# One token in eight of the gated one-hots on ScalarE, and sorted picks looked up among 8 and 16 entries

## The chip, the cores and the metric

The kernel runs on one core of a Trainium2 chip. The metric is the device time of one execution in microseconds, the median of several runs. TensorE (PE) multiplies matrices, VectorE (DVE) and ScalarE (ACT) work element by element, GpSimd (POOL) does so too and issues indirect loads, SyncE (SP) issues loads and stores. The engines run side by side, each in the order of its own instructions, and wait for each other through semaphores.

## The reference

The model is one encoder block with a gated mixer, an attention and a retrieval over 128 x 128 single-neuron experts (PEER). The change is in the retrieval alone. For 512 tokens and 8 heads two lists of 128 scores are reduced to their best 16, the sums of pairs to the best 16 pairs, and the expert is read from the two lists:

```python
s1, i1 = lax.top_k(s[:, :, 0], PEER_TOPK)
s2, i2 = lax.top_k(s[:, :, 1], PEER_TOPK)
cand = (s1[..., :, None] + s2[..., None, :]).reshape(PEER_TOKEN_BLOCK, PEER_HEADS, PEER_TOPK * PEER_TOPK)
sc, ci = lax.top_k(cand, PEER_TOPK)
e = (jnp.take_along_axis(i1, ci // PEER_TOPK, axis=-1) * N_KEYS
     + jnp.take_along_axis(i2, ci % PEER_TOPK, axis=-1))
g = jax.nn.softmax(sc, axis=-1)
u = expert_u[e]
act = jax.nn.gelu(jnp.einsum('td,thkd->thk', xb, u).astype(jnp.float32))
return jnp.einsum('thk,thkd->td', (g * act).astype(xb.dtype), expert_v[e])
```

## The kernel before

The order of each engine's instructions is that in which the program writes them; nothing reorders them later. Three of the four blocks of 128 tokens go the dense way: the hidden values of all 128 x 128 experts are computed, 128 experts at a time (a "u": a load `uraw`, its rounded part `uhi` by ScalarE, the rest `ulo` by GpSimd or, from the weights stage on, by VectorE, 24 matmuls into `pu` at L200, a GELU at L759), weighted by a table of each token's gates, and multiplied with the experts' output rows (L1007). The fourth block gathers its 128 picked experts row by row (L953 and after). `ahead(n, limit)` writes the next n matmuls of the u's between other work; `los()` writes the splits on VectorE that are due. Buffers of `uraw`, `uhi`, `ulo` and `pu` are two each.

`decode` turns the numbers of the 16 picked pairs into two lists of expert indices. The row and the column of a pair (`rw`, `cl`, 0 to 15) are copied 16 times by ScalarE (L676), compared with 0 to 15 (L683), multiplied by the sorted list's indices (L685) and summed by halves (L690, L692). It runs five times: for 3, 3 and 2 heads of the three dense blocks (n = heads x blocks = 9, 9, 6), between about 310 and 397 us, and for 4 and 4 heads of the fourth block (n = 4), between 617 and 647 us.

`turn(b)` transposes a block's indices and gates so that the 128 picks of a token lie on the partitions. The weights stage (about 400 to 545 us) then goes through 48 rounds of 8 tokens. For each, `hots` writes two one-hots of 128 per token on VectorE (`ohb`, L846, 16 rows of 128) and multiplies those of the first index with the gate, split into two 16-bit parts (`oha`, L850, 16 rows of 128). TensorE multiplies them, 16 matmuls per round (L887), to a token's table of 128 x 128 weights; ScalarE evacuates it (L867) and issues the stores. `hots` runs two rounds ahead and has three buffers of each one-hot; `acc` has four buffers, of which a round takes two. Each round has ten matmuls of u's behind its own.

The list is sorted: the pick with rank k (from 0) can only have a row or column of at most k, since every pair in front of it in both directions scores at least as high.

Of the kernel before, what the change touches and what calls it, by code (L numbers as in the profile page):

```python
# [8 lines left out]
F32 = mybir.dt.float32  # L9
# [17 lines left out]
TOPK = 16  # L27
# [17 lines left out]
def peer_block(ctx: ExitStack, tc: tile.TileContext, A, out):  # L45
# [597 lines left out]
    def decode(pool, lists, ci, outs):  # L643
# [3 lines left out]
        tl = lambda nm, dt: pool.tile(PK, dt, name=nm)  # L647

# [23 lines left out]
        wide = [128, n, TOPK, TOPK]  # L672
        ohs = []
        for r in (rw, cl):
            oh = pool.tile([128, nh, nb, TOPK, TOPK], BF16, name="oh", bufs=3 if pool is rt else 2)
            S.copy(oh.rearrange("p h b r c -> p (h b) r c"),  # L676
                   r.rearrange("p h b k -> p (h b) k")[:, :, :, None].to_broadcast(wide))
            ohs.append(oh)
        yield
        io = iota_b[:, None, None, 0:TOPK].to_broadcast(wide)  # L680
        o4 = [oh.rearrange("p h b r c -> p (h b) r c") for oh in ohs]
        for o in o4:
            V.tensor_tensor(o, o, io, op=ALU.is_equal)  # L683
        for p, o in enumerate(o4):
            V.tensor_tensor(o, o, fi.rearrange("p h b s k -> p (h b) s k")[:, :, p, None, :].to_broadcast(wide),  # L685
                            op=ALU.mult)
        yield
        for w in (8, 4, 2):
            for o in o4:
                V.tensor_tensor(o[:, :, :, 0:w], o[:, :, :, 0:w], o[:, :, :, w:2 * w], op=ALU.add)  # L690
        for oh, o in zip(ohs, outs):
            V.tensor_tensor(o, oh[:, :, :, :, 0], oh[:, :, :, :, 1], op=ALU.add)  # L692
# [15 lines left out]
    HG = (3, 3, 2)  # L708
    route = [rt.tile([128, DB, H, TOPK], F32, name=f"route{i}") for i in range(3)]
# [34 lines left out]
    def pick_head(h):  # L744
# [3 lines left out]
        for n in HG:  # L748
            if h == h0 + n - 1:
                steps.append(decode(rt, dense[1][:, h0:h0 + n], ci[:, h0:h0 + n], [r[:, h0:h0 + n] for r in by_head]))  # L750
            h0 += n
# [57 lines left out]
    def turn(b):  # L809
# [16 lines left out]
        gw = rt.tile([128, 16, 2, 8, 2], F16, name="gw", bufs=2)  # L826
        V.tensor_copy(gw[:, :, 0], gT)
        V.tensor_tensor(gw[:, :, 1], gT, gw[:, :, 0], op=ALU.subtract)
        tsc[b] = (idx, gw)
# [8 lines left out]
    def hots(t8):  # L838
# [3 lines left out]
        idx, gw = tsc[b]  # L842
# [6 lines left out]
        wide = [128, 2, 8, NK // 2, 2]  # L849
        V.tensor_tensor(a.rearrange("p (s t) (k two) -> p s t k two", s=2, two=2),  # L850
# [356 lines left out]
```

## Time and profile before

| | us |
|---|---|
| median of 3 runs | 1499.62 (1498.49 to 1500.58) |
| the profiled execution | 1503.86 |
| its span, first to last instruction | 1501.6 |
| TensorE busy | 1459.0 |
| VectorE busy | 1161.3 |
| ScalarE busy | 640.3 |
| GpSimd busy | 281.0 |

The profile is of one execution, which was a little slower than the median of the three. An engine counts as busy while an instruction of it runs. The mean granted clock of TensorE is 0.993 of full speed. In the rows below a line number is one of the kernel before; "out<-in" are the tiles that an instruction writes and reads; a releaser in brackets is what ended the engine's idle time before an instruction.

### The profile page before, as it was taken

The numbers are of one execution on the slowest core, as the hardware profiler recorded it, in microseconds if no ns is written. First come the engines' busy times: TensorE is split into PE (matmuls) and PEld (weight loads), VectorE is DVE, ScalarE is ACT, GpSimd is POOL, SyncE is SP. The second block draws the span as 40 slices with busy tenths as digits, with TensorE's granted clock in tenths as the row PEclk, the third lists the DMA queues.
The fourth block names the chain that finished last, engine by engine and source line by source line (L and its number), as shares of the span: only waits on it lengthen the run. The fifth ranks groups of instructions, "written<-read, shape, count | busy, mean of one in ns | idle before, by whom it ended". The sixth has DMA issues, their size and how long they took to land.

```text
span 1501.6 us, 21590 instructions
## 1 busy us (share of the span) xinstructions
PE 1459.0 (97%) x7945; PEld 1296.2 (86%) x7945; DVE 1161.3 (77%) x2415; ACT 640.3 (43%) x1088; POOL 281.0 (19%) x222
## 2 busy tenths in 40 slices
PE   8999999998999999899999999999999999999997
PEld 6878988888888899789999999999999999987785
DVE  4745554799999958879888888888888888877765
ACT  5455753344555543343333333333333333324334
POOL 0140002445400000012222212222212221211002
PEclk9999999999999999999999999999999999999999
DMA  6331032332366775389999999899999999988764
GB/s 218 105 101 51 22 127 91 95 95 90 113 255 265 253 274 203 105 308 354 340 338 326 331 328 336 322 327 315 337 335 322 323 321 327 324 284 292 253 199 166
DMA packets 129641, 359.31 MB, mean 239 GB/s; under 512 B 9216, under 2 KB 60672, under 8 KB 113024
## 3 DMA queue, kind: packets, MB, share of 16 engines
q1 hardware_dynamic: 104048, 198.54, 40.3%
q0 software_dynamic: 18432, 134.23, 23.6%
q10 hardware_dynamic: 7056, 25.18, 4.2%
q8 instruction: 62, 1.02, 0.3%
q14 instruction: 43, 0.35, 0.1%
HBM read 327.50 MB, written 30.41 MB: 238 GB/s over the span
## 4 chain that ended last, share of the span: by engine, by line
PE 72%; DVE 13%; DMA 7%; ACT 3%; issue 3%; POOL 1%; ACTq 0%; SPq 0%; DVEq 0%; POOLq 0%
PE pu L200 31%; PE acc L1007 27%; PE acc L251 6%; DMA vraw<-in_uv_dram 4%; DVE ohb L846 3%; DVE ulo L180 2%; DVE oha L850 2%; DVE vlo L80 1%; DMA uraw<-in_uT_dram 1%; ACT vhi L79 1%; PE tr L729 1%; PE tr L433 1%; PE pu L251 1%; POOL ulo L180 1%; PE acc L446 1%
## 5 line engine op out<-in xcount | busy, mean ns | idle before, releaser
L200 PE MATMUL pu<-h2T,uhi 128*128 128x384 f32 (+2 forms) x2336 | 452.4, 343 | 4.9 <-ACT act L759 2.4
L200 PEld LDWEIGHTS pu<-h2T,uhi 128*128 128x128 f32 x2336 | 410.6, 189 | 21.3 <-ACT uhi L169 3.0
L953 POOL DMA_INDIRECT uv<-in_uv_dram,ei x128 | 168.3, 1315 | 844.0 <-DVE xlast L968 352.0
L80 DVE TENSOR_TENSOR vlo<-vraw,vhi 128x1024 fp32r<-128x1024 f32 x128 | 156.8, 1225 | 155.7 <-ACT vhi L79 155.7
L79 ACT CAST vhi<-vraw 128x1024 fp32r<-128x1024 f32 x128 | 134.6, 1051 | 287.2 <-issue 174.7
L200 PE MATMUL pu<-h2T,ulo 128*128 128x384 f32 (+2 forms) x1168 | 236.2, 342 | 7.4 <-DVE ulo L180 5.2
L1007 PE MATMUL acc<-vhi,wahi 128*128 128x512 f32 x768 | 239.4, 392 | 2.2 <-ACT wahi L79 2.2
L1007 PE MATMUL acc<-vlo,wahi 128*128 128x512 f32 x768 | 239.1, 392 | 0.4
L1007 PE MATMUL acc<-vhi,walo 128*128 128x512 f32 x768 | 238.2, 391 | 0.0
L200 PEld LDWEIGHTS pu<-h2T,ulo 128*128 128x128 f32 x1168 | 204.9, 189 | 13.8 <-DVE ulo L180 6.4
L169 ACT CAST uhi<-uraw 128x1024 fp32r<-128x1024 f32 x144 | 150.7, 1047 | 63.1 <-DMA uraw<-in_uT_dram 49.8
L1007 PEld LDWEIGHTS acc<-vlo,wahi 128*128 128x128 f32 x768 | 144.4, 189 | 33.9 <-DVE vlo L80 2.4
L1007 PEld LDWEIGHTS acc<-vhi,walo 128*128 128x128 f32 x768 | 144.2, 188 | 31.6 <-DVE walo L80 0.7
L968 DVE SCALAR_TENSOR_TENSOR xlast<-uv,dot,xlast 128x1024 f32<-128x1024 f32 x128 | 164.5, 1285 | 4.5
L1007 PEld LDWEIGHTS acc<-vhi,wahi 128*128 128x128 f32 x768 | 143.2, 188 | 27.3 <-ACT wahi L79 3.5
L959 DVE SCALAR_TENSOR_TENSOR uv<-uv,h 128x1024 f32<-128x1024 f32 x128 | 153.7, 1219 | 9.5 <-DMA uv<-in_uv_dram,ei 9.5
L180 DVE TENSOR_TENSOR ulo<-uraw,uhi 128x1024 fp32r<-128x1024 f32 x116 | 141.6, 1220 | 22.6 <-ACT uhi L169 22.3
L759 ACT ACTIVATE act<-pu 128x384 f32<-128x384 f32 x128 | 62.9, 491 | 220.6 <-PE pu L200 220.2
L180 POOL TENSOR_TENSOR ulo<-uraw,uhi 128x512 fp32r<-128x512 f32 x56 | 81.3, 1475 | 209.3 <-PE acc L251 106.3
L79 ACT CAST wahi<-wa 128x384 fp32r<-128x384 f32 x128 | 65.3, 510 | 41.2 <-DVE wa L992 41.2
L992 DVE TENSOR_TENSOR wa<-act,wt 128x384 f32<-128x384 f32 x128 | 70.6, 551 | 2.2 <-DMA wt<-wd 2.1
L80 DVE TENSOR_TENSOR walo<-wa,wahi 128x384 fp32r<-128x384 f32 x128 | 70.7, 553 | 0.6 <-ACT wahi L79 0.6
(250 smaller groups left out, 1475.7 us busy)
## 6 DMA issues: line engine op xcount, KB each, us to landing
uraw<-in_uT_dram SPq DMA_DIRECT2D x128, 512.0 KB, 6.1
vraw<-in_uv_dram SPq DMA_DIRECT2D x128, 512.0 KB, 5.6
wd<-wst ACTq DMA_DIRECT2D x48, 512.0 KB, 2.8
wt<-wd SPq DMA_DIRECT2D x32, 768.0 KB, 11.2
wraw<-in_w_in_dram SPq DMA_DIRECT2D x19, 512.0 KB, 3.7
uraw<-in_w_q_dram SPq DMA_DIRECT2D x16, 512.0 KB, 3.8
xT<-in_xT_dram SPq DMA_DIRECT2D x8, 256.0 KB, 3.7
xt<-in_x_dram SPq DMA_DIRECT2D x1, 2048.0 KB
```

The lines of the kernel that those rows point to most:

```text
L79: S.copy(hi, src)
L80: sub.tensor_tensor(lo, src, hi.bitcast(F32), op=ALU.subtract)
L169: S.copy(hi, raws[i])
L180: eng.tensor_tensor(lo[:, k, :], raws[i][:, k, :], hi[:, k, :].bitcast(F32), op=ALU.subtract)
L200: T.matmul(o, l[:, k, :], r[:, k, t0:n], start=(p == 0 and k == 0), stop=(p == 2 and k == KT - 1))
L251: T.matmul(out[b], l[:, b * 128:(b + 1) * 128], r[:, kk, :], start=(k == 0 and i == 0), stop=(k == KT - 1 and i == 2))
L759: S.activation(acts[e], o[:, :DT], AF.Gelu_apprx_tanh)
L953: G.indirect_dma_start(out=uvs[r].rearrange("p s d -> p (s d)"), out_offset=None, in_=A["uv"], in_offset=bass.IndirectOffsetOnAxis(ap=ei[: ...
L959: V.scalar_tensor_tensor(uv[:, 0, :], uv[:, 0, :], 1.0, h2, op0=ALU.mult, op1=ALU.mult, accum_out=d[:, 0:1])
L968: V.scalar_tensor_tensor(xlast, uv[:, 1, :], d[:, 1:2], xlast, op0=ALU.mult, op1=ALU.add)
L992: eng.tensor_tensor(wa.rearrange("p (c t) -> p c t", c=NWC), acts.pop(e).rearrange("p (c t) -> p c t", c=NWC), wts[e // WG][:, :, e % WG, ...
L1007: T.matmul(acc[b][n], l[:, c], r[:, n * 512:(n + 1) * 512], start=(e == 0 and i == 0), stop=(e == NK - 1 and i == 2))
```

## The change

`decode`: the compare, multiply and sum of a pick go over 8 entries of the list instead of 16, and for the picks 8 to 15 a second group of 8 entries follows. A tile has 24 rows of 8 (rows 0 to 15 for entries 0 to 7 of all picks, rows 16 to 23 for entries 8 to 15 of the last 8 picks) in place of 16 rows of 16. The numbers to compare with lie in a tile made once per pool by `lookup_rows` on GpSimd. ScalarE's copy and VectorE's multiply become two instructions each.

`hots`: VectorE multiplies the one-hots of seven of the eight tokens; those of the eighth are made by ScalarE in `gated`, two activations of 128 columns per round with the gate as a scale per partition, behind the round's evacuation and GELU. The rows of `oha` are ordered by token and then by part. `turn` orders `gw` so too and writes the eighth token's scales in float32 (`gs`).

```diff
--- before.py
+++ after.py
@@ -640,11 +640,19 @@
             pos += na * nb_
         return cand
 
-    def decode(pool, lists, ci, outs):
+    def lookup_rows(pool):
+
+        rows = pool.tile([128, 24, 8], BF16, name="iota_v")
+        for r0, r1, c0 in ((0, 16, 0), (16, 24, 8)):
+            G.tensor_copy(rows[:, r0:r1, :], iota[:, None, c0:c0 + 8].to_broadcast([128, r1 - r0, 8]))
+        return rows
+
+    def decode(pool, iota_v, lists, ci, outs):
 
         _, nh, nb, _ = PK = list(ci.shape)
         n = nh * nb
         tl = lambda nm, dt: pool.tile(PK, dt, name=nm)
+        K8 = TOPK // 2
 
         cf, at = tl("cf", F16), tl("at", F16)
         mks = [tl(f"mk{i}", F16) for i in range(3)]
@@ -669,27 +677,33 @@
         V.tensor_copy(fi, lists)
         yield
         yield
-        wide = [128, n, TOPK, TOPK]
-        ohs = []
+
+
+        o4 = []
         for r in (rw, cl):
-            oh = pool.tile([128, nh, nb, TOPK, TOPK], BF16, name="oh", bufs=3 if pool is rt else 2)
-            S.copy(oh.rearrange("p h b r c -> p (h b) r c"),
-                   r.rearrange("p h b k -> p (h b) k")[:, :, :, None].to_broadcast(wide))
-            ohs.append(oh)
+            oh = pool.tile([128, n, TOPK + K8, K8], BF16, name="oh", bufs=3 if pool is rt else 2)
+            flat = r.rearrange("p h b k -> p (h b) k")[:, :, :, None]
+            S.copy(oh[:, :, 0:TOPK, :], flat.to_broadcast([128, n, TOPK, K8]))
+            S.copy(oh[:, :, TOPK:, :], flat[:, :, K8:, :].to_broadcast([128, n, K8, K8]))
+            o4.append(oh)
         yield
-        io = iota_b[:, None, None, 0:TOPK].to_broadcast(wide)
-        o4 = [oh.rearrange("p h b r c -> p (h b) r c") for oh in ohs]
         for o in o4:
-            V.tensor_tensor(o, o, io, op=ALU.is_equal)
+            V.tensor_tensor(o, o, iota_v[:, None, :, :].to_broadcast([128, n, TOPK + K8, K8]), op=ALU.is_equal)
         for p, o in enumerate(o4):
-            V.tensor_tensor(o, o, fi.rearrange("p h b s k -> p (h b) s k")[:, :, p, None, :].to_broadcast(wide),
+            f = fi.rearrange("p h b s k -> p (h b) s k")[:, :, p, None, :]
+            V.tensor_tensor(o[:, :, TOPK:, :], o[:, :, TOPK:, :], f[:, :, :, K8:].to_broadcast([128, n, K8, K8]),
+                            op=ALU.mult)
+            V.tensor_tensor(o[:, :, 0:TOPK, :], o[:, :, 0:TOPK, :], f[:, :, :, 0:K8].to_broadcast([128, n, TOPK, K8]),
                             op=ALU.mult)
         yield
-        for w in (8, 4, 2):
+        for o in o4:
+            V.tensor_tensor(o[:, :, K8:TOPK, :], o[:, :, K8:TOPK, :], o[:, :, TOPK:, :], op=ALU.add)
+        for w in (4, 2):
             for o in o4:
-                V.tensor_tensor(o[:, :, :, 0:w], o[:, :, :, 0:w], o[:, :, :, w:2 * w], op=ALU.add)
-        for oh, o in zip(ohs, outs):
-            V.tensor_tensor(o, oh[:, :, :, :, 0], oh[:, :, :, :, 1], op=ALU.add)
+                V.tensor_tensor(o[:, :, 0:TOPK, 0:w], o[:, :, 0:TOPK, 0:w], o[:, :, 0:TOPK, w:2 * w], op=ALU.add)
+        for o, dst in zip(o4, outs):
+            o = o.rearrange("p (h b) k c -> p h b k c", h=nh)
+            V.tensor_tensor(dst, o[:, :, :, 0:TOPK, 0], o[:, :, :, 0:TOPK, 1], op=ALU.add)
         yield
 
     def softmax(pool, top, g):
@@ -706,6 +720,7 @@
         yield
 
     HG = (3, 3, 2)
+    iota_v = lookup_rows(rt)
     route = [rt.tile([128, DB, H, TOPK], F32, name=f"route{i}") for i in range(3)]
     by_head = [r.rearrange("p b h k -> p h b k") for r in route]
     top = rt.tile([128, H, DB, TOPK], F32, name="top")
@@ -747,7 +762,7 @@
         h0 = 0
         for n in HG:
             if h == h0 + n - 1:
-                steps.append(decode(rt, dense[1][:, h0:h0 + n], ci[:, h0:h0 + n], [r[:, h0:h0 + n] for r in by_head]))
+                steps.append(decode(rt, iota_v, dense[1][:, h0:h0 + n], ci[:, h0:h0 + n], [r[:, h0:h0 + n] for r in by_head]))
             h0 += n
 
     acts = {}
@@ -823,10 +838,14 @@
         gT = rows[2]
         yield
 
-        gw = rt.tile([128, 16, 2, 8, 2], F16, name="gw", bufs=2)
-        V.tensor_copy(gw[:, :, 0], gT)
-        V.tensor_tensor(gw[:, :, 1], gT, gw[:, :, 0], op=ALU.subtract)
-        tsc[b] = (idx, gw)
+        gw = rt.tile([128, 16, 8, 2, 2], F16, name="gw", bufs=2)
+        V.tensor_copy(gw[:, :, :, 0], gT)
+        V.tensor_tensor(gw[:, :, :, 1], gT, gw[:, :, :, 0], op=ALU.subtract)
+
+        gs = rt.tile([128, 16, 2], F32, name="gs", bufs=2)
+        V.tensor_copy(gs[:, :, 0], gw[:, :, 7, 0, 0])
+        V.tensor_tensor(gs[:, :, 1], gT[:, :, 7, 0], gs[:, :, 0], op=ALU.subtract)
+        tsc[b] = (idx, gw, gs)
         yield
 
     drain(turn(0))
@@ -839,23 +858,33 @@
 
 
         b, g = divmod(t8, 16)
-        idx, gw = tsc[b]
+        idx, gw, gs = tsc[b]
         pairs = lambda t: t.rearrange("p s t two -> p (s t) two")[:, :, None, :].to_broadcast(half)
         c = rt.tile([128, 16, NK], BF16, name="ohb", bufs=3)
         a = rt.tile([128, 16, NK], F16, name="oha", tag="oh", bufs=3)
         V.tensor_tensor(c.rearrange("p s (k two) -> p s k two", two=2),
                         iota_b.rearrange("p (k two) -> p k two", two=2)[:, None, :, :].to_broadcast(half),
                         pairs(idx[:, g]), op=ALU.is_equal)
-        wide = [128, 2, 8, NK // 2, 2]
-        V.tensor_tensor(a.rearrange("p (s t) (k two) -> p s t k two", s=2, two=2),
-                        c[:, None, 8:16].rearrange("p o t (k two) -> p o t k two", two=2).to_broadcast(wide),
-                        gw[:, g, :, :, None, :].to_broadcast(wide), op=ALU.mult)
+        wide = [128, 7, 2, NK // 2, 2]
+        V.tensor_tensor(a[:, 0:14].rearrange("p (t s) (k two) -> p t s k two", s=2, two=2),
+                        c[:, 8:15, None].rearrange("p t o (k two) -> p t o k two", two=2).to_broadcast(wide),
+                        gw[:, g, 0:7, :, None, :].to_broadcast(wide), op=ALU.mult)
+        rest.append((a, c, gs, g))
         return a, c
+
+    rest = []
+
+    def gated():
+        for a, c, gs, g in rest:
+            for s in range(2):
+                S.activation(a[:, 14 + s, :], c[:, 15, :], AF.Copy, scale=gs[:, g, s:s + 1])
+        rest.clear()
 
     N8 = DT // 8
     per = WTOK // 8
     wst = None
     hot = [hots(0), hots(1)]
+    gated()
     ahead(24, AHEAD)
     los()
     flush()
@@ -884,7 +913,7 @@
             for j in range(4):
                 for s in range(2):
                     t = 4 * q + j
-                    T.matmul(pw[:, j, :], c[:, t, :], a[:, 8 * s + t, :], start=(s == 0), stop=(s == 1))
+                    T.matmul(pw[:, j, :], c[:, t, :], a[:, 2 * t + s, :], start=(s == 0), stop=(s == 1))
             t0 = (t8 % per) * 8 + 4 * q
             new.append((pw, wst[:, :, t0:t0 + 4]))
         ahead((t8 + 1) * left // N8 - t8 * left // N8, AHEAD)
@@ -899,6 +928,7 @@
         evac.extend(new)
         put()
         flush()
+        gated()
         if t8 % per == per - 1:
             full = (t8 // per, wst)
         if full is not None and t8 + 1 < N8:
@@ -920,6 +950,8 @@
     ei = gp.tile([128, 128], I32, name="ei")
     late = (gp.tile([128, H, 1, 2, TOPK], F32, name="gs16"), gp.tile([128, H, 1, 2, TOPK], U32, name="gi16"))
     h2 = gp.tile([128, 1024], F32, name="h2")
+
+    iota_g = lookup_rows(gp)
 
     def gather_routing():
 
@@ -940,7 +972,7 @@
         for h in range(0, H, 4):
             next(gating, None)
             next(gating, None)
-            yield from decode(gp, late[1][:, h:h + 4], gci[:, h:h + 4], [r[:, h:h + 4] for r in groute])
+            yield from decode(gp, iota_g, late[1][:, h:h + 4], gci[:, h:h + 4], [r[:, h:h + 4] for r in groute])
         fl = lambda t: t.rearrange("p h b k -> p (h b k)")
         V.scalar_tensor_tensor(fl(groute[0]), fl(groute[0]), float(NK), fl(groute[1]), op0=ALU.mult, op1=ALU.add)
         V.tensor_copy(ei, fl(groute[0]))
```

## Rows read from the trace of the kernel before

**Rows 1.** Busy us of each engine over the whole span, from the page.

```profile
PE 1459.0 (97%) x7945; PEld 1296.2 (86%) x7945; DVE 1161.3 (77%) x2415; ACT 640.3 (43%) x1088; POOL 281.0 (19%) x222
```

**Rows 2.** Stretches: start:end, length, busy of PE, PEld, DVE, ACT, POOL; clock, DMA.

```profile
331.00:400.00 69.00, 62.15 (x337) 58.42 (x336) 66.14 (x289) 33.46 (x41) 41.94 (x26) 0.98 0.32 104
...
403.00:540.00 137.00, 130.94 (x1233) 120.74 (x1233) 134.87 (x118) 80.32 (x139) 0.00 (x0) 1.00 0.66 243
...
545.00:660.00 115.00, 107.63 (x536) 98.57 (x537) 84.83 (x353) 44.87 (x62) 3.94 (x4) 0.97 0.59 199
...
660.00:1335.00 675.00, 675.00 (x3414) 614.55 (x3413) 557.88 (x789) 247.82 (x440) 155.10 (x115) 1.00 0.93 329
```

**Rows 3.** Groups of the weights stage, 403 to 540 us: busy us, mean ns.

```profile
L850 DVE TENSOR_TENSOR oha<-ohb,gw 128x2048 f16<-128x2048 bf16 x47 | 57.6, 1225 | 1.6
...
L846 DVE TENSOR_TENSOR ohb<-iota_b,idxT 128x2048 bf16<-128x2048 bf16 x47 | 57.3, 1218 | 0.0
...
L180 DVE TENSOR_TENSOR ulo<-uraw,uhi 128x1024 fp32r<-128x1024 f32 x20 | 24.4, 1219 | 0.0
```

**Rows 4.** Timeline of VectorE in the weights stage: start us, length us.

```profile
400.46 1.22 DVE L846 TENSOR_TENSOR ohb<-iota_b,idxT 128x2048 bf16<-128x2048 bf16 x1
...
404.11 1.23 DVE L850 TENSOR_TENSOR oha<-ohb,gw 128x2048 f16<-128x2048 bf16 x1
...
405.25 1.22 DVE L180 TENSOR_TENSOR ulo<-uraw,uhi 128x1024 fp32r<-128x1024 f32 x1
...
406.39 1.22 DVE L846 TENSOR_TENSOR ohb<-iota_b,idxT 128x2048 bf16<-128x2048 bf16 x1
...
407.64 1.22 DVE L850 TENSOR_TENSOR oha<-ohb,gw 128x2048 f16<-128x2048 bf16 x1
...
538.32 1.23 DVE L850 TENSOR_TENSOR oha<-ohb,gw 128x2048 f16<-128x2048 bf16 x1
```

**Rows 5.** Timeline of TensorE: products behind a wait, in brackets its length and releaser.

```profile
359.53 4.63 PE L200 MATMUL pu<-h2T,uhi 128*128 128x384 f32 x16 [2.40 <-ACT act L759]
...
374.47 0.98 PE L200 MATMUL pu<-h2T,ulo 128*128 128x384 f32 x4 [1.98 <-POOL ulo L180]
...
397.22 0.33 PE L815 MATMUL po<-ident,route 128*128 128x128 f32 x1 [1.53 <-DVE route L692]
...
639.55 2.93 PE L200 MATMUL pu<-h2T,ulo 128*128 128x384 f32 x8 [2.02 <-DVE ulo L180]
...
659.34 1.68 PE L200 MATMUL pu<-h2T,ulo 128*128 128x384 f32 x8 [1.35 <-DVE ulo L180]
```

**Rows 6.** Groups of VectorE's decodes, 310 to 400 and 545 to 660 us.

```profile
L683 DVE TENSOR_TENSOR oh<-oh,iota_b 128x2304 bf16<-128x2304 bf16 x4 | 5.3, 1362 | 0.0
...
L683 DVE TENSOR_TENSOR oh<-oh,iota_b 128x1024 bf16<-128x1024 bf16 x4 | 2.6, 686 | 0.0
...
L690 DVE TENSOR_TENSOR oh<-oh 128x512 bf16<-128x512 bf16 x4 | 1.5, 421 | 0.0
```

**Rows 7.** Groups of ScalarE over the whole span.

```profile
L820 ACT ACTIVATE idxT<-po 128x256 bf16<-128x256 f32 x3 | 1.1, 380 | 6.4 <-PE po L815 6.4
...
L269 ACT ACTIVATE qraw<-acc,xrs 128x512 f32<-128x512 f32 x7 | 4.3, 688 | 0.3 <-DVE xrs L146 0.3
...
L676 ACT CAST oh<-rw 128x2304 bf16<-128x2304 int32 x2 | 4.2, 2112 | 1.8 <-DVE rw L666 1.8
```

**Rows 8.** Timeline of GpSimd's splits, and VectorE's sums of the last decode.

```profile
253.06 2.53 POOL L180 TENSOR_TENSOR ulo<-uraw,uhi 128x512 fp32r<-128x512 f32 x2 [13.02 <-ACT uhi L169]
...
366.48 12.02 POOL L180 TENSOR_TENSOR ulo<-uraw,uhi 128x512 fp32r<-128x512 f32 x4 [2.31 <-ACT uhi L169]
...
388.63 7.08 POOL L180 TENSOR_TENSOR ulo<-uraw,uhi 128x512 fp32r<-128x512 f32 x4 [2.92 <-ACT uhi L169]
...
391.36 5.32 DVE L690 TENSOR_TENSOR oh<-oh 128x768 bf16<-128x768 bf16 x6
```

## The prediction

> **What bounds the kernel now.** I read the page's busy shares first. TensorE is busy for 1459.0 of 1501.6 us [rows 1], so there are about 43 us to be had in all, and the question is which of them lie where the diff works. The table by stretches answers that [rows 2]. From 660 to 1335 us TensorE is busy in every microsecond: whatever is won before 660 us arrives there as an earlier start and is neither enlarged nor lost. Idle TensorE that the diff can reach lies in three places: 6.9 us in 331 to 400 (the routing's decodes), 6.1 us in 403 to 540 (the weights stage with its 48 rounds of one-hots), 7.4 us in 545 to 660 (the gather routing).
>
> In the weights stage VectorE is busy for 134.9 of 137 us, TensorE for 130.9, ScalarE for 80.3 [rows 2]. The groups of this stage say what VectorE does: 47 of the 48 one-hots of 1.218 us, as many gated ones of 1.225 us, 20 `ulo` splits of 1.219 us [rows 3]. The timeline shows them back to back: a gated one-hot at 404.11, a split at 405.25, the next one-hot at 406.39, its gated one at 407.64 [rows 4]. So a gated one-hot holds VectorE for 1.14 us and a pair for 2.39. 48 pairs and 20 splits of 1.14 make 138 us, and from the first one-hot at 400.46 to the last gated one's end at 539.55 there are 139.1 [rows 4]. VectorE sets this stage. Its instructions are the lever, and TensorE's own work stands close behind.
>
> In 331 to 400 VectorE is busy for 66.1 of 69 us [rows 2], and three of TensorE's waits end on something that stands behind a decode: 2.40 us at 359.53 on a GELU that sits behind the decode's casts in ScalarE's queue, 1.98 at 374.47 on a split of GpSimd, 1.53 at 397.22 on the decode's last sum [rows 5]. In 545 to 660, the 2.02 us at 639.55 and the 1.35 us at 659.34 end on a VectorE split that stands in the queue behind the gather decodes [rows 5].
>
> **The change, part by part.**
>
> *The gated one-hots (`hots`).* The multiply writes 14 rows of 128 where it wrote 16, so 256 elements fewer. VectorE's price of an element comes from the lookups' compares: 2304 elements 1362 ns, 1024 elements 686 ns, so 0.528 ns each and 0.145 us fixed [rows 6]. 256 elements are 0.135 us, times 48 is 6.5 us. The new order of the rows (token, then part) keeps the inner pair of adjacent 16-bit values and the number of loops, so I let it run at the same price; if it lost that, a multiply would about double. That is a rival below.
>
> *The scale columns (`gs` in `turn`).* Two VectorE instructions of 16 elements per block of tokens. No row shows them. They cost at least next to nothing and at most what 512 elements cost, 0.42 us [rows 6]; I take the fixed part, 0.15 each, since they have hardly any elements. One block stands ahead of the stage (0.3 us), two within it (0.6). The other order of `gw` changes no element count: nothing, bounded by the same 0.42.
>
> *The token on ScalarE (`gated`).* Two activations of 128 elements in each round, 96 in all. The nearest rows are 256 elements without a scale column, 380 ns, and 512 with one, 688 [rows 7]. With the cast of 2304 in 2112 ns as the third, an element is (2112 − 380)/2048 = 0.85 ns, so 128 elements with a column are 688 − 384 × 0.85 = 0.36 us; the lower bound is 0.27 (380 less 128 elements, no column), the upper the 0.688 itself. I take 0.36, since the row with the column is the same kind of instruction. 96 of them are 35 us, and ScalarE goes from 80 to about 115 of some 132 us. It has room, so I cost them at nothing. What hides them is its waiting for the accumulators.
>
> The Trainium skill (ScalarE: Activation LUTs, What ACT_TABLE_LOAD costs) gives 186 ns and 0.833 ns per element, and 93 ns more for a pointer operand: by it one would take 386 ns and the 96 some 37 us, an estimate. The trace's difference between the two forms bears this out, and the sum is the same by either.
>
> The pair adds a wait: it stands behind the evacuation and the GELU of its round and waits for the one-hot of two rounds later. Behind it in ScalarE's queue are the store of the weights, the next `uhi` cast and the next evacuation. The evacuation has time until the accumulator is used again two rounds later (four buffers, two per round). The cast is needed by a split that VectorE reaches only after another pair of one-hots. TensorE needs the pair for its last two products of the round alone. With 2.7 us per round none of this is late; without the cover it costs what the rival says.
>
> *How much of it the stage gives back.* VectorE loses 6.5 and gains 0.6: 5.9 us less. TensorE's idle time caps it at 6.1 [rows 2]. After the change the two engines need almost the same time, and with the splits in some rounds and not in others one or the other is a little late: I take 5.3, bounds 3.5 and 6.1.
>
> *The lookups in `decode`, on the way into the stage.* For each of two lists with n = 9 the elements are before 2304 + 2304 + 1152 + 576 + 288 + 144, after 1728 + 576 + 1152 + 576 + 576 + 288 + 144: 1728 fewer, 0.91 us. One instruction more per list costs its fixed part less the overlap of about 0.08 that the rows show between a 1.22 us instruction and the next one's start 1.14 later: 0.07. So 1.7 us per decode; with n = 6 it is 1152 elements, 1.1 us. Three decodes make 4.5 us less on a VectorE that is 96% busy. ScalarE's cast is split in two and drops 576 elements of 2304: 0.49 less for the elements, about 0.1 more for the second instruction, 0.4 us per list for n = 9. The cover of these times is thin, as the three waits show, and a shorter decode also frees GpSimd: its four splits took 12.02 us from 366.48 on and 7.08 from 388.63 on [rows 8], while the same decodes ran on VectorE, whose three pairs of sums took 5.32 us from 391.36 on. If all of the 4.5 arrived, the stage would start 4.2 earlier, with 0.3 for `gs`; the path also goes through the loads of `uraw` and GpSimd, which don't get faster by themselves. TensorE's waits there are 5.9 us together. I take 3.0; bounds minus 2 (the rival on GpSimd) and 5.
>
> *The gather's decodes.* n = 4: 768 elements fewer per list, 0.41 us, less 0.07. Two lists and two decodes: 1.35 us. They stand on the way to the gather, and the split that TensorE waits for at 659.34 stands behind the first gathered row. I take 1.3. The lower bound is 0. The upper is 2.6: at 639.55 eight products took 2.93 us, at 659.34 as many took 1.68 [rows 5]; the first ran, after a wait of 2.02, at about the lower of the clock's two levels, 1.2 GHz, in a stretch whose granted clock is 0.97 on the mean [rows 2], and a wait shorter by 0.7 might spare that.
>
> *The tables (`lookup_rows`).* Four small copies on GpSimd. The first two come ahead of the split at 253.06, before which GpSimd had waited for 13.02 us [rows 8]. The other two come at the end of the weights stage, in which it has no instruction [rows 2]. Nothing; uncovered, at most four times 1.77, the mean of the splits from 388.63.
>
> **Sum.** 5.3 + 3.0 + 1.3 = 9.6 us. The profiled execution took 1503.86 us around its span of 1501.6; it would take 1494.3. It stands 4.24 above the median of the three runs, 1499.62, so the median goes to **1490.0**. A measurement tells about 0.2%, 3.0 us, from no change.
>
> **Rivals.**
> 1. *The way into the stage is held by loads and GpSimd.* The uhi cast ahead of the transposes waits for its load, and the load for GpSimd's split, so a shorter decode only makes VectorE wait. For it: TensorE's wait at 374.47 is on GpSimd. Against: GpSimd was slow just when the decode ran. Then 6.6 us less: 1493.0.
> 2. *GpSimd takes the gain of the decodes.* A decode has two two-input instructions more. If each of them waits for one split of GpSimd (1.77 us on the mean [rows 8]), three decodes lose 10.6 and save 4.5, 6.1 more on the way in; if half of them wait, it is 0.8 more. Between the two, at 2 us, the change is worth 5.3 − 2 + 1.3 = 4.6, and the time is 1495. The Trainium skill (GPSIMD Engine Reference, Specifications) says that GpSimd's SBUF interfaces are shared with VectorE and contended by instructions with two SBUF inputs. The 5.32 us for six sums that by their 2688 elements and 0.07 each need 1.8 agree [rows 6, 8].
> 3. *ScalarE becomes the bound (slower).* It has 137 − 80 = 57 us free, of which TensorE's pace takes 6: 1.06 us per round. If the pair, with what it waits for in order, holds the queue for longer than that, each round is late by the excess. At 1.35 us the stage is 14 us longer than TensorE needs and 8 longer than now; with 4.3 won outside it the time is 1503. For it: the pair waits for VectorE, and the casts stand behind it. Against: a pair is 0.72 us.
> 4. *The multiply loses its rate.* 1792 elements at twice 0.528: 0.95 more each, less the 0.135, is 39 us in 48 rounds; with the 4.3 from outside the stage, 1534. The number of loops and the inner pair speak against it.
> 5. *Nothing to be seen.* TensorE can't use the time in the stage and rival 1 or 2 holds ahead of it: 1497 to 1499.
>
> **Chances and range.** Forecast 0.52, rival 1 0.23, rival 2 0.07, rival 3 0.07, rival 4 0.03, rival 5 0.08. Faster by over 0.2%: the forecast and the first two rivals but for a small part, 0.81. Slower: 0.09. Within: 0.10. The range goes from 1484 (6.1, 5 and 2.6 us, and a little beyond for clock regained) to 1498, where rivals 1, 2 and part of 5 are in it.
>
> **What the profile after would show.** The gated one-hot on VectorE takes 1.09 us; two activations per round of 0.36 us appear on ScalarE, busy for about 115 us of the stage. From the first one-hot to the last there are about 134 us, TensorE is busy in 97% or more of it, and the waits on `oha` shrink. The first one-hot starts at about 397.5 instead of 400.46. The gather decode's six sums and four lookups are 0.65 us shorter. It is wrong if TensorE waits for ScalarE's rows of the gated one-hot, if `ulo` on VectorE waits for `uhi`, or if the first one-hot starts no earlier.

## The result and the profile after

The changed kernel takes 1490.63 us (median of 6 runs, 1487.97 to 1491.67) against 1500.06 of the kernel before on the same chip (6 runs): a ratio of 0.9935, 95% interval 0.9924 to 0.9947. The forecast of 1490.0 and its sign hold. The profiled execution has a span of 1489.7 us.

The busy times and the four stretches of the changed kernel, beside [rows 1] and [rows 2] (columns as there; the stretches are laid up to 10 us earlier, because the work is):

```profile
PE 1454.2 (98%) x7945; PEld 1293.7 (87%) x7945; DVE 1151.1 (77%) x2431; ACT 661.9 (44%) x1194; POOL 280.9 (19%) x226
```

```profile
331.00:396.00 65.00, 60.84 (x334) 57.45 (x333) 62.34 (x279) 31.66 (x44) 40.85 (x26) 0.97 0.35 110
396.00:535.00 139.00, 136.51 (x1280) 127.66 (x1280) 132.78 (x128) 107.30 (x240) 0.88 (x1) 1.00 0.66 247
535.00:650.00 115.00, 107.74 (x545) 97.64 (x543) 82.70 (x357) 44.33 (x65) 4.46 (x6) 0.99 0.60 206
650.00:1325.00 675.00, 675.00 (x3413) 614.95 (x3414) 557.58 (x789) 248.58 (x441) 154.26 (x115) 1.00 0.92 329
```

TensorE's idle time in the weights stage fell from 6.1 us of 137 to 2.5 of 139. The last stretch is as full as it was, so what was won ahead of it stays won.

The groups of the weights stage in the changed kernel, 390 to 545 us, beside [rows 3]: busy us, mean ns of one, idle time ahead of them.

```profile
L865 DVE TENSOR_TENSOR ohb<-iota_b,idxT 128x2048 bf16<-128x2048 bf16 x48 | 58.4, 1217 | 0.0
L869 DVE TENSOR_TENSOR oha<-ohb,gw 128x1792 f16<-128x1792 bf16 x48 | 52.4, 1092 | 1.6
L880 ACT ACTIVATE oha<-ohb,gs 128x128 f16<-128x128 bf16 x96 | 33.5, 400 | 27.8 <-DVE ohb L865 27.8
```

The multiply went from 1225 to 1092 ns, so the new order of the rows kept its rate. ScalarE's rows take 400 ns each, and ScalarE still spends 27.8 us waiting for the one-hots they are made from: it has room.

Where the stage begins, VectorE's timeline of the changed kernel (start us, length us; [rows 4] before):

```profile
396.44 0.59 DVE L842 CAST gw<-gT 128x256 f16<-128x256 f32 x1 [2.37 <-ACT gT L835]
397.07 0.42 DVE L843 TENSOR_TENSOR gw<-gT,gw 128x256 f16<-128x256 f32 x1
397.41 0.17 DVE L846 CAST gs<-gw 128x16 f32<-128x16 f16 x1
397.61 0.18 DVE L847 TENSOR_TENSOR gs<-gT,gs 128x16 f32<-128x16 f32 x1
397.71 1.21 DVE L865 TENSOR_TENSOR ohb<-iota_b,idxT 128x2048 bf16<-128x2048 bf16 x1
...
530.55 1.09 DVE L869 TENSOR_TENSOR oha<-ohb,gw 128x1792 f16<-128x1792 bf16 x1
```

The first one-hot starts at 397.71 where it started at 400.46, and the last gated one ends at 531.64 where it ended at 539.55: 133.9 us in place of 139.1.

TensorE's waits in the changed kernel (start, length; in brackets the wait and its releaser), which answer to [rows 5]:

```profile
358.67 3.07 PE L200 MATMUL pu<-h2T,uhi 128*128 128x384 f32 x16 [0.91 <-ACT act L774]
372.60 2.89 PE L200 MATMUL pu<-h2T,ulo 128*128 128x384 f32 x8 [2.53 <-POOL ulo L180]
395.66 0.33 PE L830 MATMUL tr<-ident,route 128*128 128x128 f32 x1 [0.64 <-ACT idxT L835]
...
537.93 3.05 PE L200 MATMUL pu<-h2T,uhi 128*128 128x384 f32 x16 [0.95 <-ACT uhi L169]
...
631.11 1.70 PE L200 MATMUL pu<-h2T,ulo 128*128 128x384 f32 x8 [1.77 <-DVE ulo L180]
649.99 1.68 PE L200 MATMUL pu<-h2T,ulo 128*128 128x384 f32 x8 [0.39 <-DVE ulo L180]
```

The wait of 2.40 us for a GELU is 0.91 now, that of 1.53 for the decode's last sum is gone, and that for a split of GpSimd grew from 1.98 to 2.53. The wait of 0.95 behind the stage was 0.50.

The eight products near 631 take 1.70 us, where those of before took 2.93 at the lower clock. But the slow products are only others now. Of those right behind the eight, the second pair takes 1.05 us in the changed kernel (first line) and 0.63 in the kernel before:

```profile
633.46 1.05 PE L1039 MATMUL acc<-vlo,wahi 128*128 128x512 f32 x2
...
643.05 0.63 PE L1007 MATMUL acc<-vlo,wahi 128*128 128x512 f32 x2
```

From the start of the eight to the next u's first product there are 7.17 us before (639.55 to 646.72) and 7.23 in the changed kernel (631.11 to 638.34), so nothing was won there.

TensorE's waits for VectorE's gated one-hots, 403 to 530 us, in the kernel before and in the changed one, and VectorE's one wait in the changed one (total us, times, longest):

```profile
PE acc L887 <- DVE oha L850: 3.4, 9, 0.5
...
PE acc L916 <- DVE oha L869: 0.8, 1, 0.8
...
DVE ulo L180 <- ACT uhi L169: 0.6, 1, 0.6
```

For the accounts below each trace is cut at marks. The first is the start of the last eight products with the keys, near 345 us: it moves by up to 3.0 us between kernels whose instructions are the same up to there, as the time behind the last u does by 3.7. So a section is compared from that mark on. All times are us:

| kernel | key product to first one-hot | first one-hot to last gated one | to TensorE's next wait for `uhi` | from there to the expert indices | key product to the last wait for `ulo` |
|---|---|---|---|---|---|
| before | 54.79 | 139.09 | 5.85 | 102.13 | 313.67 |
| changed | 51.42 | 133.93 | 6.29 | 100.48 | 303.70 |
| one-hots only | 55.15 | 133.91 | 6.40 | 102.08 | 308.54 |
| decodes only | 51.19 | 139.06 | 5.86 | 100.44 | 308.13 |

From that last wait for `ulo` to the start of the last GELU of a u it is 674.55 or 674.56 us in all four.

### The profile page after: what moved, and what is told of

It is laid out like the page before. It is cut to its first block, busy times and chain, and to the rows that moved or that the text cites. A ratio compares the mean times of both kernels' runs of the same rounds, so it can differ in the third digit from the quotient of the medians.

```text
span 1489.7 us, 21734 instructions
## 1 busy us (share of the span) xinstructions
PE 1454.2 (98%) x7945; PEld 1293.7 (87%) x7945; DVE 1151.1 (77%) x2431; ACT 661.9 (44%) x1194; POOL 280.9 (19%) x226
## 4 chain that ended last, share of the span: by engine, by line
PE 73%; DVE 13%; DMA 5%; ACT 4%; issue 3%; POOL 0%; ACTq 0%; SPq 0%; DVEq 0%; POOLq 0%
PE pu L200 32%; PE acc L1039 27%; PE acc L251 6%; DMA vraw<-in_uv_dram 3%; DVE ohb L865 3%; DVE ulo L180 2%; DVE oha L869 1%; DVE vlo L80 1%; PE tr L744 1%; PE tr L433 1%; PE pu L251 1%; PE acc L446 1%; ACT vhi L79 1%; ACT uhi L169 1%; PE po L446 1%
## 5 line engine op out<-in xcount | busy, mean ns | idle before, releaser
L80 DVE TENSOR_TENSOR vlo<-vraw,vhi 128x1024 fp32r<-128x1024 f32 x128 | 156.8, 1225 | 155.4 <-ACT vhi L79 155.4
## 6 DMA issues: line engine op xcount, KB each, us to landing
wt<-wd SPq DMA_DIRECT2D x32, 768.0 KB, 11.6
xt<-in_x_dram SPq DMA_DIRECT2D x1, 2048.0 KB, 10.4
```

What stands on the lines that cost most here:

```text
L80: sub.tensor_tensor(lo, src, hi.bitcast(F32), op=ALU.subtract)
```

## The experiments

**The two parts, and the two kinds of decode, each alone.** e1_hots_only is the changed kernel with the `decode` of before (and no `lookup_rows`); e2_decode_only is the kernel before with the new `decode` everywhere; e6_dense_decode_only and e7_gather_decode_only have it in the three dense decodes, or in the gather's two, with the one-hots of before.

```diff
--- after.py
+++ e1_hots_only.py
-            V.tensor_tensor(o, o, iota_v[:, None, :, :].to_broadcast([128, n, TOPK + K8, K8]), op=ALU.is_equal)
+            V.tensor_tensor(o, o, io, op=ALU.is_equal)
...
-        for w in (4, 2):
+        for w in (8, 4, 2):
...
--- after.py
+++ e2_decode_only.py
-        wide = [128, 7, 2, NK // 2, 2]
+        wide = [128, 2, 8, NK // 2, 2]
...
-        gated()
--- e2_decode_only.py
+++ e6_dense_decode_only.py
-            yield from decode(gp, iota_g, late[1][:, h:h + 4], gci[:, h:h + 4], [r[:, h:h + 4] for r in groute])
+            yield from decode_old(gp, late[1][:, h:h + 4], gci[:, h:h + 4], [r[:, h:h + 4] for r in groute])
--- e2_decode_only.py
+++ e7_gather_decode_only.py
-                steps.append(decode(rt, iota_v, dense[1][:, h0:h0 + n], ci[:, h0:h0 + n], [r[:, h0:h0 + n] for r in by_head]))
+                steps.append(decode_old(rt, dense[1][:, h0:h0 + n], ci[:, h0:h0 + n], [r[:, h0:h0 + n] for r in by_head]))
```

> The changed kernel with the decode of before: only the gated one-hots, gw and gs are changed. Theory (VectorE set the weights stage and gives its shorter multiply back until TensorE sets it): the stage is 5.2 us shorter and starts 0.3 later than before, the kernel is about 5 us faster than before, 1495. Rival (TensorE set the stage, the whole gain came from the decodes): 1499.5 to 1500.

> The kernel of before with only the decode (lookups among 8 and 16 entries) changed, the one-hots as before. Theory: about 3 us from the way into the weights stage and 1.3 from the gather's decodes, 4.3 in all, 1495.7. Rival (loads and GpSimd hold the way in): only the gather's 1.3, 1498.7. Rival (GpSimd takes back more than is saved): no gain or slower, 1500 or more.

> The kernel of before with the new lookups in the dense blocks' three decodes alone. Theory: the first one-hot starts 3.6 us earlier after the last key product, as with all five decodes, and the whole is 3.6 us faster than before, about 1496.4. Rival (the earlier start is given back by waits on loads behind it): 1498.5 to 1500 with the first one-hot as early.

> The kernel of before with the new lookups in the fourth block's two decodes alone. Theory: from the end of the weights stage to the gather's indices 1.3 to 1.7 us less, and as much in the whole, about 1498.5. Rival (the gathered rows' loads hide it): no change, 1500.

| kernel | us | before | ratio (95%) |
|---|---|---|---|
| e1_hots_only | 1495.21 | 1499.98 | 0.9973 (0.9963 to 0.9983) |
| e2_decode_only | 1494.23 | 1499.98 | 0.9960 (0.9947 to 0.9973) |
| e6_dense_decode_only | 1495.51 | 1499.61 | 0.9976 (0.9966 to 0.9985) |
| e7_gather_decode_only | 1497.34 | 1499.61 | 0.9986 (0.9977 to 0.9994) |

The parts add up to within 0.7 us. By the marks e1 gains 313.67 − 308.54 = 5.1 us and e2 5.5, together 10.7 beside the 10.0 of the whole change. Of the first four columns e6 moves only the first (51.19), e7 only the fourth (100.41). So the shorter dense decodes do reach TensorE, and each part's gain stays in its own stage. What lies between the indices and the last wait for `ulo` takes 11.8 us before, 11.6 in the changed kernel, 11.0 in e1 and 10.4 in e6. This spread is not explained; by it e6 gains 4.9 us to the last mark, where its column gained 3.6.

**ScalarE's rows: none, two tokens, three tokens, and a lighter VectorE.** e3_no_scalar_rows leaves ScalarE's two activations out (the eighth token's products read the seventh's rows); e4_two_tokens and e9_three_tokens give ScalarE two and three tokens of eight, and VectorE the rest; e5_six_on_vector lets VectorE write 12 rows and ScalarE two (the seventh token's products read the sixth's rows).

```diff
--- after.py
+++ e3_no_scalar_rows.py
-                S.activation(a[:, 14 + s, :], c[:, 15, :], AF.Copy, scale=gs[:, g, s:s + 1])
+                pass
...
-                    T.matmul(pw[:, j, :], c[:, t, :], a[:, 2 * t + s, :], start=(s == 0), stop=(s == 1))
+                    T.matmul(pw[:, j, :], c[:, t, :], a[:, 2 * min(t, 6) + s, :], start=(s == 0), stop=(s == 1))
--- after.py
+++ e4_two_tokens.py
-        wide = [128, 7, 2, NK // 2, 2]
+        wide = [128, 6, 2, NK // 2, 2]
...
-            for s in range(2):
-                S.activation(a[:, 14 + s, :], c[:, 15, :], AF.Copy, scale=gs[:, g, s:s + 1])
+            for t in range(2):
+                for s in range(2):
+                    S.activation(a[:, 12 + 2 * t + s, :], c[:, 14 + t, :], AF.Copy, scale=gs[:, g, t, s:s + 1])
--- after.py
+++ e9_three_tokens.py
-        wide = [128, 7, 2, NK // 2, 2]
+        wide = [128, 5, 2, NK // 2, 2]
...
-            for s in range(2):
+            for t in range(3):
+                for s in range(2):
+                    S.activation(a[:, 10 + 2 * t + s, :], c[:, 13 + t, :], AF.Copy, scale=gs[:, g, t, s:s + 1])
--- after.py
+++ e5_six_on_vector.py
-        wide = [128, 7, 2, NK // 2, 2]
+        wide = [128, 6, 2, NK // 2, 2]
...
-                    T.matmul(pw[:, j, :], c[:, t, :], a[:, 2 * t + s, :], start=(s == 0), stop=(s == 1))
+                    T.matmul(pw[:, j, :], c[:, t, :], a[:, 2 * (5 if t == 6 else t) + s, :], start=(s == 0), stop=(s == 1))
```

> The changed kernel without ScalarE's pair: the eighth token's gated one-hots are not made, and its products read the seventh token's (left out: one token in eight of the weights). Theory (the pair hides in ScalarE's room): within 1.5 us of the changed kernel, 1489 to 1491. Rival (the pair costs, through the order of ScalarE's queue): 3 us or more faster than the changed kernel, 1487 or less.

> Two tokens in eight made by ScalarE, four activations a round, 12 rows left to VectorE. Theory (ScalarE's room ends at about 1.06 us a round): ScalarE needs 107 + 33 = 140 us of a stage in which TensorE needs 131, so ScalarE sets it and the kernel is 6 to 10 us slower than the changed one, 1497 to 1501. Rival (ScalarE has room, VectorE still sets the stage): 2 us or more faster than the changed one, 1488.

> Three tokens in eight made by ScalarE, six activations a round. With two the four took 1.28 us a round and the stage was no longer. Theory (ScalarE's queue, at about 0.32 us for each further one, runs out of room between two and three): 80 + 48 x 1.93 = 173 us less the overlap of about 15, so a stage of 150 to 160 us, 1505 to 1517. Rival (there is room for three too): 1489 to 1491.

> The changed kernel with VectorE's multiply cut to 12 rows and ScalarE's pair as it is; the seventh token's products read the sixth's rows (left out: one token in eight of the weights). Theory (TensorE sets the stage after the change): the stage, 133.9 us from the first one-hot to the last gated one, falls by 1 to 1.5 us and no more, though VectorE has 6.5 less to do. Rival (VectorE still sets it): 6 us less, 1484.

| kernel | us | ratio (95%) | first to last product of the weights (TensorE) |
|---|---|---|---|
| changed | 1490.63 | 0.9935 (0.9924 to 0.9947) | 132.66 |
| e3_no_scalar_rows | 1487.93 | 0.9924 (0.9911 to 0.9936) | 131.76 |
| e5_six_on_vector | 1487.23 | 0.9917 (0.9904 to 0.9930) | 131.12 |
| e4_two_tokens | 1489.42 | 0.9934 (0.9922 to 0.9947) | 132.46 |
| e9_three_tokens | 1516.30 | 1.0112 (1.0098 to 1.0127) | 158.43 |

The stretch from 403 to 530 us of e4, e5 and e9, in this order, one line of each table (columns as in [rows 2]; the changed kernel has VectorE at 125.33 and ScalarE at 101.42 there):

```profile
403.00:530.00 127.00, 124.16 (x1193) 116.33 (x1192) 119.34 (x119) 125.31 (x321) 0.00 (x0) 1.00 0.72 261
```

```profile
403.00:530.00 127.00, 125.10 (x1200) 117.67 (x1200) 118.50 (x118) 103.83 (x231) 0.00 (x0) 1.00 0.72 265
```

```profile
403.00:530.00 127.00, 117.64 (x987) 101.46 (x986) 97.51 (x102) 125.22 (x341) 0.00 (x0) 0.99 0.59 213
```

My theory for e4, that ScalarE would become the bound, fell: it is busy for 125.31 of 127 us and the time is that of the changed kernel. ScalarE's timeline says how the four fit:

```profile
442.54 1.28 ACT L881 ACTIVATE oha<-ohb,gs 128x128 f16<-128x128 bf16 x4
443.72 1.05 ACT L169 CAST uhi<-uraw 128x1024 fp32r<-128x1024 f32 x1
```

From the first of the four activations to the start of the next instruction there are 1.18 us, 0.295 each, where one alone takes 0.40. But the second pair is not free. e4 and e5 leave VectorE the same 12 rows, and e4's stage is 1.3 us longer (132.46 and 131.12). In e4 TensorE waits once for ScalarE's rows (403 to 530 us: total, times, longest):

```profile
PE acc L917 <- ACT oha L881: 1.2, 1, 1.2
```

So what VectorE's lighter multiply could give in e4 is taken back. With the third token the room is used up. The longest wait of e9 (403 to 540 us) is one that the prediction named as a sign of being wrong, on a cast that stands behind ScalarE's rows:

```profile
DVE ulo L180 <- ACT uhi L169: 29.5, 16, 3.6
```

So rival 3's mechanism is real, its point lies between two and three tokens, and the change is on this side of it. e5 shows where TensorE sets the end: VectorE has 8.5 us to spare in 127 there, and on TensorE the stage is only 1.5 us shorter than in the changed kernel. (On VectorE, by which I had expected 1 to 1.5, it is 3.8 shorter, 130.1 from the first one-hot to the last gated one, since VectorE runs ahead.) e3 prices the pair at 0.9 us in the stage, and behind the stage the wait for `uhi` is 0.51 instead of 0.95. Its median lies between my two forecasts for it; by the last wait for `ulo`, 302.36 us from the key product, the pair costs 1.3 in all.

**The last stores on another queue.** Behind the stage ScalarE issues four stores of the weights (3.20 us in the changed kernel) ahead of the `uhi` cast that TensorE waits 0.95 us for. e10_stores_on_sp lets SyncE issue those four; e11_two_tokens_sp does so in e4.

```diff
--- after.py
+++ e10_stores_on_sp.py
-    def store(j):
+    def store(j, q=S):
...
-        S.dma_start(wd[full[0], :, j * n:(j + 1) * n, :], full[1][:, j * n:(j + 1) * n, :])
+        q.dma_start(wd[full[0], :, j * n:(j + 1) * n, :], full[1][:, j * n:(j + 1) * n, :])
...
-        store(j)
+        store(j, Q)
```

> The changed kernel with the last four stores of the weights issued by SyncE instead of ScalarE. They hold ScalarE for 3.3 us behind the last evacuation, and the next rounded part waits for that; TensorE then waits 0.95 us (0.50 before the change). Theory (the change's pair pushed ScalarE's last evacuations back, and that wait reaches the end): the wait is gone and the kernel is 0.5 to 1 us faster than the changed one, 1489.7 to 1490.1. Rival (SyncE's loads behind the stores come later and give it back): 1491 or more.

> Two tokens made by ScalarE (stage as long as with one) and the last four stores issued by SyncE. Theory: with TensorE as the bound of the stage no more than 1.5 us are left in it; 1488.5 to 1490. Rival: ScalarE is too full for two tokens and the stores' move changes nothing, 1490.6 or more.

e10 takes 1492.42 us, a ratio of 0.9961 (0.9947 to 0.9974) to 1498.67; e11 1493.10, also 0.9961 (0.9947 to 0.9974). Both are slower than without the move: from the key product to the last wait for `ulo` e10 takes 3.4 us more than the changed kernel, e11 3.0 more than e4. SyncE's queue in e10 shows why, and TensorE's next two u's behind it:

```profile
531.29 2.86 SPq L904 DMA_DIRECT2D wd<-wst  x4
534.26 9.26 SPq L162 DMA_DIRECT2D uraw<-in_uT_dram  x3
```

```profile
534.54 2.93 PE L200 MATMUL pu<-h2T,uhi 128*128 128x384 f32 x16
...
541.97 4.61 PE L200 MATMUL pu<-h2T,uhi 128*128 128x384 f32 x16 [3.10 <-ACT uhi L169]
```

And the same three loads on SyncE's queue in the changed kernel, and the second of the two u's (the first, at 537.93, is shown above):

```profile
529.40 11.42 SPq L162 DMA_DIRECT2D uraw<-in_uT_dram  x3
```

```profile
542.20 2.94 PE L200 MATMUL pu<-h2T,uhi 128*128 128x384 f32 x16
```

The first of the two u's waits for nothing in e10 and starts 1.1 us sooner after the key product: the wait of 0.95 is gone, as the theory had it. But the three loads of `uraw` stand behind the stores. They begin at 534.26 and not at 529.40, though the key product of this run of e10 was 2.3 us earlier: 7.2 us late. So the second u, which waited for nothing, waits 3.10 us, and takes 4.61 in place of 2.94.

**Small two-input instructions in the dense decodes.** Rival 2 put the price of a two-input instruction of VectorE at one split of GpSimd, whatever its size. e12_small_ops adds twelve of 16 elements.

```diff
--- after.py
+++ e12_small_ops.py
                             op=ALU.mult)
+            for _ in range(2 if pool is rt else 0):
+                V.tensor_tensor(cf[:, 0, 0, :], cf[:, 0, 0, :], at[:, 0, 0, :], op=ALU.add)
         yield
```

> The changed kernel with four more two-input instructions of VectorE in each dense decode, two behind each of the two lists' first multiply. Each adds 16 elements per partition in a tile that is not read again, so the output stays as it is. In the three decodes they are 12. Theory (what VectorE's decode costs goes by its elements, and GpSimd's splits are stretched by how long VectorE's two-input instructions run, not by how many there are): about 0.1 us each, so the first one-hot starts at most 1.2 us later after the last key product than in the changed kernel (51.42 us there), and GpSimd's splits beside the decodes keep their lengths within 0.5 us; the time rises by 1 us, which a measurement hardly tells from nothing. Rival (each two-input instruction waits for a split of GpSimd, whatever its size, as the prediction's second rival has it): up to 1.77 us for each that meets a split, which half of the 12 may do; the first one-hot starts 4 us or more later, and the time rises by as much.

It takes 1493.31 us, a ratio of 0.9964 (0.9950 to 0.9978), where the change has 0.9935; the first one-hot starts 54.63 us after the key product, 3.2 later than in the changed kernel, between what the theory allowed (1.2) and what the rival asked (4). The group of the added instructions in e12 (total us, mean ns), and those of the second decode in VectorE's timeline:

```profile
L699 DVE TENSOR_TENSOR cf<-cf,at 128x16 f16<-128x16 f16 x12 | 10.6, 881 | 0.2
```

```profile
364.75 0.75 DVE L696 TENSOR_TENSOR oh<-oh,fi 128x1152 bf16<-128x1152 bf16 x1
365.42 2.51 DVE L699 TENSOR_TENSOR cf<-cf,at 128x16 f16<-128x16 f16 x2
367.86 0.45 DVE L694 TENSOR_TENSOR oh<-oh,fi 128x576 bf16<-128x576 bf16 x1
368.23 1.84 DVE L696 TENSOR_TENSOR oh<-oh,fi 128x1152 bf16<-128x1152 bf16 x1
```

The shortest of the twelve takes 0.165 us, the median 1.218, the longest 1.267. Sixteen elements can cost as much as a GpSimd split, two of which in a row take 2.5 us. My theory, that the elements set the price, falls. But the number of instructions doesn't set it either. In the third decode e12 has four instructions more and takes 10.03 us from the first compare to the last sum, where the changed kernel takes 9.80. The added ones, one multiply and the sums of that decode:

```profile
388.00 2.51 DVE L699 TENSOR_TENSOR cf<-cf,at 128x16 f16<-128x16 f16 x2
...
390.69 1.64 DVE L696 TENSOR_TENSOR oh<-oh,fi 128x768 bf16<-128x768 bf16 x1
392.26 1.45 DVE L699 TENSOR_TENSOR cf<-cf,at 128x16 f16<-128x16 f16 x2
...
394.16 1.12 DVE L705 TENSOR_TENSOR oh<-oh 128x384 bf16<-128x384 bf16 x4
```

Three of the added instructions and one multiply are stretched there, by 1.1 us each, and the sums are not. In the changed kernel two multiplies and two sums of that decode are stretched, in the kernel before one multiply and three sums, by as much. That is four each time, one for each of GpSimd's four splits beside that decode. So rival 2 has the price of one wait right, and its count, one wait for each instruction more, is wrong: in these decodes the splits set the count.

What e12 pays, it pays in the second decode, which takes 11.75 us in place of 6.84. There the four splits got shorter, 7.64 us, than in the changed kernel:

```profile
365.74 10.86 POOL L180 TENSOR_TENSOR ulo<-uraw,uhi 128x512 fp32r<-128x512 f32 x4 [2.41 <-ACT uhi L169]
```

Most of the 10.86 us is a single split, which is held while VectorE's decode runs. By itself, in the changed kernel and in the kernel before:

```profile
365.74 6.80 POOL L180 TENSOR_TENSOR ulo<-uraw,uhi 128x512 fp32r<-128x512 f32 x1 [2.41 <-ACT uhi L169]
...
366.48 7.94 POOL L180 TENSOR_TENSOR ulo<-uraw,uhi 128x512 fp32r<-128x512 f32 x1 [2.31 <-ACT uhi L169]
```

In both it ends 1.1 us behind the decode's last sum, so a decode that ends sooner frees GpSimd as much sooner. In e12 that split ends after 3.1 us, and four of VectorE's instructions are stretched in its place. What lets GpSimd in there was not tried. The Trainium skill (GPSIMD Engine Reference, Specifications) says that GpSimd shares its SBUF interfaces with VectorE and that instructions with two SBUF inputs contend for them; the traces agree, with some 1.1 us for each split. They show it for instructions with one input too. In the kernel before, two of VectorE's of one size, the first of them beside a split from 377.21 to 378.50:

```profile
377.35 1.19 DVE L652 TENSOR_SCALAR mk<-cf 128x96 f16<-128x96 f16 x1
378.46 0.17 DVE L655 TENSOR_SCALAR mk<-cf 128x96 f16<-128x96 f16 x1
```

## Why the prediction was right, point by point

**The stage.** Predicted 5.3 less, measured 139.09 − 133.93 = 5.2 on VectorE, and 5.0 on TensorE (137.68 from first to last product before, 132.66 after). A multiply lost 0.133 us (1225 to 1092 ns), where 0.135 was worked out. TensorE's waits for a gated one-hot shrank from 3.4 us to 0.8, and a still lighter VectorE gives 1.5 us more and no more (e5): the two engines need almost the same time, as was predicted.

**ScalarE.** One row took 400 ns, not 360, and ScalarE was busy for 107 us of the stage, not 115. (The Trainium skill, ScalarE: Activation LUTs, What ACT_TABLE_LOAD costs, by whose figures one takes 386 ns, an estimate, was nearer than my rows.) That it costs nothing was nearly right: e3 says 0.9 us in the stage. Of the three signs of being wrong one did occur, a wait of `ulo` for `uhi`, once and for 0.6 us. What I missed stands behind it: with the pair, ScalarE's last evacuations end later, the next `uhi` too, and 0.4 us is given back (the column to the next wait for `uhi`, 5.85 to 6.29; e1 has 6.40, e2 and e3 none of it).

**Rival 3's point.** I put it at 1.06 us per round, from busy times. e4's four rows take 1.18 per round, which by that sum is 6 us too much, and cost 1.3 over e5, since instructions in a row start 0.1 us closer together than they are long. Room that is counted in lengths is counted too small.

**The way in.** Predicted 3.0 with `gs`, measured 54.79 − 51.42 = 3.4, with `gs` at 0.17 and 0.18 as taken. The second decode is 1.8 us shorter (8.63 us from its first compare to its last sum before, 6.84 after), the third 1.1 (10.89 to 9.80), as the elements said. The rest of what arrived, 0.8, is there when the second decode begins. Its first compare starts 18.9 to 19.0 us after the key product in the three kernels with the old dense decodes, and 18.1 to 18.3 in nine of the ten with the new (17.5 in e11). What differs on VectorE ahead of it is the first decode, so the 0.8 is put down to that. What it gained ahead of the mark can't be told from the mark's spread. The gain reaches TensorE by the split that was held: the products behind it start 26.3 us after the key product where they started 28.8. The first two copies for the tables cost nothing, as taken: GpSimd waits 4.76 us behind them.

**Rivals 1 and 2.** Rival 1 falls with e6: dense decodes alone reach the first one-hot in full. Rival 2's single wait is real, and its sum was right to be refused. VectorE's timeline of the changed kernel's last decode shows the price being paid:

```profile
386.08 0.35 DVE L694 TENSOR_TENSOR oh<-oh,fi 128x384 bf16<-128x384 bf16 x1
386.35 0.55 DVE L696 TENSOR_TENSOR oh<-oh,fi 128x768 bf16<-128x768 bf16 x1
386.82 1.45 DVE L694 TENSOR_TENSOR oh<-oh,fi 128x384 bf16<-128x384 bf16 x1
388.19 1.64 DVE L696 TENSOR_TENSOR oh<-oh,fi 128x768 bf16<-128x768 bf16 x1
389.75 0.61 DVE L700 TENSOR_TENSOR oh<-oh 128x384 bf16<-128x384 bf16 x2
390.29 3.29 DVE L703 TENSOR_TENSOR oh<-oh 128x384 bf16<-128x384 bf16 x4
```

The same two instructions take 0.35 and 0.55 us, then 1.45 and 1.64. But the kernel before paid as much in its last decode (six sums in 5.32 us, [rows 8]), four stretched instructions for four splits in both, so the difference is that of the elements. In the second decode no instruction of VectorE is stretched, and GpSimd paid. The 12.02 us of [rows 8] were not four slow splits, as the prediction took them, but one of 7.94 and three of 1.28 to 1.63.

**The gather.** Predicted 1.3, measured 102.13 − 100.48 = 1.65, and e7 alone 1.7. The two decodes are 1.44 us shorter from their first compare to their last sum (4.39 to 3.64 and 7.53 to 6.84), where 1.35 was worked out; the other 0.2 is not accounted for. The clock that was named as an upper bound did not come back near 631 us: the lower clock only fell on other products.

**The sum.** 5.2 + 3.4 + 1.65, less the 0.4 given back behind the stage, is 9.7; with 0.2 between the indices and the last wait for `ulo` it is 10.0 by the marks (313.67 − 303.70) against 9.6 predicted; the medians say 9.4. The terms are right to 0.4 us each, and the misses partly cancel. That the median of 1490.63 lies within 0.6 us of the forecast is partly luck, with runs from 1487.97 to 1491.67.

## What to carry to other kernels

Where one engine sets a stage and a second has only a few us to spare in it, the gain of a lighter instruction is its elements times their rate up to the second engine's floor, and no further. Count an idle engine's room in starts of instructions in a row, and test it with twice the load: here the second token's rows cost 1.3 us and the third's 26. Ahead of moving a few issues to a quiet queue, look at which loads stand behind them. When a group of instructions is slow on the mean, look at each: here one split of four held nearly all of the loss.

## What the runs showed of the hardware

A two-input instruction of VectorE with 16 elements took 0.165 us alone and up to 1.27 beside GpSimd's splits, and a one-input one of 96 elements 1.19 in place of 0.17. In the third decode of three kernels four of VectorE's instructions were stretched beside four splits, however many there were. In the second decode a split waited instead: 6.80 us behind a decode of 6.84, and 7.94 behind one of 8.63. What decides who waits was not tried. ScalarE's activation of 128 elements with a scale column takes 0.40 us, and four in a row 1.28.
